# Moving a weight-splitting subtraction from VectorE to GpSimd in the mixer of a one-core decoder step

## The chip, the core and the metric

The kernel runs on one core of one Trainium2 chip. Its time is the device time of one execution in microseconds (us); runs are told by their median. The engines are named as in the profile: PE (TensorE's matmuls), PEld (its weight loads), DVE (VectorE), ACT (ScalarE), POOL (GpSimd) and SP (the queue that issues all DMAs here). Every engine works through its own instructions strictly in the order of the program, so an instruction that waits holds up all that stand behind it on that engine.

## The reference

One step of a decoder layer for 1024 prompt tokens and 8 sample tokens (D = 1024, feed-forward width 2816). The four parts follow each other, each with a residual and a layer norm:

```python
h = LN(ALPHA * h + 0.5 * swiglu(h, ffn1_wi, ffn1_wo))
proj = h @ w_in                      # 58 column tiles of 128
# RWKV-7 branch: token shift, decay, in-context rates, matrix state per head, read out in chunks of 64
# RG-LRU branch: causal convolution of width 4, gates, linear scan, GeLU gate
merged = gate0 * rwkv_out + gate1 * lru_out
h = LN(ALPHA * h + merged @ w_mix_out)
h = LN(ALPHA * h + cross_attention(h, mem_k, mem_v))
h = LN(ALPHA * h + 0.5 * swiglu(h, ffn2_wi, ffn2_wo))
```

All values are float32, and the results must have close to float32 precision.

## The kernel before

Every large product is made of three matmuls (`mm3`, lines 125 to 127): both operands are split into a rounded high part and the rest, and high x high, high x low and low x high are added up in PSUM. So every weight tile must be split before PE can use it. `split_half` does this for half a tile (128 x 512 values): SP loads it into a tile `raw` (line 94), ACT rounds it to `wh` (line 99), DVE subtracts to get `wl` (line 100), and PE takes `wh` and `wl` as the stationary operand. Nothing else sets the pace of the split: the next load into `raw` waits until `wl` is made.

The mixer is the middle part of the program. It first makes the low-rank inputs of the RWKV branch; then (from line 734 on) it works in 16 units, two for each of 8 pairs of heads. In each unit `rounds` interleaves, step by step and in the order of the code, several streams:

- `gemms`: the products with the remaining 52 tiles of `w_in`, in three column groups of 344 tokens (PSUM tile `g`), whose results go out to DRAM as `ev`; in the last two units `out_proj` with the 8 tiles of `w_mix` takes its place;
- `chain`: the recurrence over chunks of 64 tokens. One chunk is a closed chain of PE and DVE (L1049 PE, L1051 DVE `wsb`, L1055 PE, L1061 DVE and an ACT copy into `QZ`, L1065 and L1067 PE, L549 DVE `QZ<-y`), and the next chunk needs its result;
- `inverse`: 31 rounds of a DVE product (`pr<-tq,iv`) and a DVE reduction (L900) that need no PE at all;
- `stage`, `branch`, `post`, `samples_*`: elementwise work for the next unit and the finished one, with small POOL instructions (a power for each norm, L754 `ivs` and `ivc`, and a copy, L845 `BN`).

In this stretch the weights have one `raw` buffer and three pairs of `wh` and `wl`. After the 16 units the last chain, the second part of the output product (`out_last`), the layer norm, the memory's keys and values (`memory_kv`) and the first queries of the attention are interleaved. The scheduler that builds the program may change the order of neighbouring instructions, by its own estimates of when each is ready.

Of the kernel before, what the change touches and what calls it, by code (L numbers as in the profile page):

```python
# [10 lines left out]
F32 = mybir.dt.float32  # L11
F32R = mybir.dt.float32r
AF = mybir.ActivationFunctionType
ALU = mybir.AluOpType
# [20 lines left out]
def weave(*streams):  # L35

    live = [[0.0, i, g, 1.0 / n] for i, (g, n) in enumerate((s if isinstance(s, tuple) else (s, 1) for s in streams))]
    while live:
        x = min(live, key=lambda v: v[:2])
        try:  # L40
            new = next(x[2])
            x[0] += x[3]
            if new:
                live.append([x[0], len(streams), new[0], (1.0 - min(x[0], 0.9)) / new[1]])
        except StopIteration:
            live.remove(x)


def rounds(n, streams, late, keep):


    done = [0] * len(streams)
    for r in range(1, n + 1):
        for g in late[:]:
            try:
                next(g)
            except StopIteration:
                late.remove(g)
        for i, (g, steps) in enumerate(streams):
            while done[i] < steps and (done[i] < steps * r // n or r == n):  # L60
                done[i] += 1
                try:
                    new = next(g)
                    if new:
                        late.append(new[0])
                except StopIteration:
                    done[i] = steps
    for g, steps in streams:
        for new in g:
            if new:  # L70
                late.append(new[0])
    while late and not keep:
        for g in late[:]:
            if next(g, 0) == 0:
                late.remove(g)
# [10 lines left out]
def raw_tile(S):  # L86
    return next(S.rawseq).tile([128, 2 * HN], F32, tag="raw", name="raw")


def split_half(S, src, nm="w", hp=None, view=lambda t: t, to=None):  # L90

    nc = S.nc
    raw = raw_tile(S)[:, :512]
    S.wdma.dma_start(out=view(raw), in_=src)
    if to is None:
        hp = hp or next(S.hlseq)
        to = [hp.tile([128, 512], F32R, tag=nm + x, name=nm + x) for x in "hl"]
    hi, lo = to
    nc.scalar.activation(out=hi, in_=raw, func=AF.Identity)  # L99
    nc.vector.tensor_tensor(out=lo, in0=raw, in1=hi.bitcast(F32), op=ALU.subtract)  # L100
    return hi, lo


def load_split(S, src, nm="w", hp=None):

    return [split_half(S, src[:, 512 * i:512 * i + 512], nm, hp) for i in range(2)]
# [368 lines left out]
def setup(ctx, tc, I):  # L475
    nc = tc.nc
    S = SimpleNamespace(tc=tc, nc=nc, pend=[])
    S.const = ctx.enter_context(tc.tile_pool(name="const", bufs=1))
    S.hp = ctx.enter_context(tc.tile_pool(name="hp", bufs=1))
    S.wraw = ctx.enter_context(tc.tile_pool(name="wraw", bufs=1))  # L480
    S.whl = ctx.enter_context(tc.tile_pool(name="whl", bufs=3))
    S.wdma = nc.sync
    S.dram = ctx.enter_context(tc.tile_pool(name="dram", bufs=1, space=bass.MemoryType.DRAM))
    S.ones_d = S.const.tile([128, 128], F32, name="ones_d")
    nc.vector.memset(S.ones_d, 1.0 / D)
    S.lng = S.const.tile([128, 4, KT], F32, name="lng")
    S.lnb = S.const.tile([128, 4, KT], F32, name="lnb")
    nc.sync.dma_start(out=S.lng, in_=I["ln_g"])
    nc.sync.dma_start(out=S.lnb, in_=I["ln_b"])
    S.mhalf = S.const.tile([128, 8], F32, name="mhalf")  # L490
    nc.vector.memset(S.mhalf, -0.5)
    S.ident = S.const.tile([128, 128], F32, name="ident")
    nc.sync.dma_start(out=S.ident, in_=I["cst"][:, 0:128])
    S.HH = S.hp.tile([128, KT, NT], F32R, name="HH")
    S.HL = S.hp.tile([128, KT, NT], F32R, name="HL")
    return S
# [42 lines left out]
def mixer(octx, S, I, O, MG, HD, pre):  # L539
# [5 lines left out]
    nc, tc = S.nc, S.tc  # L545
# [7 lines left out]
    with ExitStack() as ctx:  # L553
# [107 lines left out]
        with ExitStack() as c2:  # L661
# [64 lines left out]
            def rest():  # L726
                for x in tiles(0)[2:4]:
                    yield from project(0, *x, load_split(S, I["w_in"][x[0]]), CH3, psl, lp)
                ends(0, True)

            weave((first(), 31), *pre)
            weave((low_out(), 29), (rest(), 17))
        S.norms.close()
        S.rawseq, S.hlseq = itertools.cycle([S.wraw]), itertools.cycle([S.whl])

        pools.update(dict.fromkeys(("g", "ch", "y"), ctx.enter_context(tc.tile_pool(name="mps", bufs=1, space=PSUM))))
# [7 lines left out]
        def tmp(tag, n=264, bufs=1, pool=None):  # L744
            return (pool or (t1 if tag in LATE else ta)).tile([128, n], F32, tag=tag, name=tag, bufs=bufs)
# [252 lines left out]
        def direct(k, c0, n, e):  # L998

            ACT(S.HH[:, k, c0:c0 + n], e)  # L1000
            TTo(S.HL[:, k, c0:c0 + n], e, S.HH[:, k, c0:c0 + n].bitcast(F32), ALU.subtract)
# [132 lines left out]
        def samples_c(p, P):  # L1134

            col = lambda t: t[:, p:p + 1]
            y, sg = P.y8, P.sg
            e0 = tmp("e0", 8, 2, t1)
            nc.sync.dma_start(out=e0, in_=GD[p][:, G0, NP:NT])
            while len(P.lm) < 4:  # L1140
                yield
            v = tmp("w8", 8, 2, t1)
            q = psm(8)
            nc.tensor.matmul(q, ones64, y, start=True, stop=True)
            TTo(y, y, q, ALU.subtract)
            ACT(v, y, AF.Square)
            yield
            q = psm(8)
            nc.tensor.matmul(q, ones64, v, start=True, stop=True)
            TSC(v, q, GN_EPS, None, ALU.add, None)  # L1150
            nc.gpsimd.tensor_tensor(out=v, in0=v, in1=mhalf, op=ALU.pow)
            STT(sg[:, 1, :], e0, 1.0, sg[:, 1, :], ALU.add, ALU.mult)
            yield
            yield
            STT(y, y, col(V["gng"]), v, ALU.mult, ALU.mult)
            STT(y, y, col(V["gnb"]), sg[:, 0, :], ALU.add, ALU.add)
            STT(y, y, 0.5, sg[:, 1, :], ALU.mult, ALU.mult)
            STT(y, sg[:, 2, :], 0.5, y, ALU.mult, ALU.add)
            if p < S.npairs - 1:
                nc.sync.dma_start(out=MG[p, :, NP:NT], in_=y)  # L1160
            else:
                direct(p, NP, NS, y)
# [75 lines left out]
        for t in range(nu):  # L1238
# [21 lines left out]
            if t == nu - 1:  # L1260
                s.append((out_proj(range(4, 8), KT - 1, (KT - 2,)), 37))
            rounds(26, s, late_steps, t < nu - 2)
        weave(samples_c(S.npairs - 1, Ps[-1]))
        actx.close()
        S.norms = Norms(S, octx)
        more_weights(S, ctx, 2, 1)
        wp = ctx.enter_context(tc.tile_pool(name="wmix", bufs=3))
        fp = ctx.enter_context(tc.tile_pool(name="fmix", bufs=2))
        w = [[split_half(S, I["w_mix"][4 * i:4 * i + 4, :, 128 * k:128 * k + 128].rearrange("m p c -> p m c"), hp=wp,
                         view=lambda t: t.rearrange("p (m c) -> p m c", c=128)) for i in range(2 if k == KT - 1 else 1)]  # L1270
             for k in (KT - 2, KT - 1)]
# [21 lines left out]
def memory_kv(S, ctx, I, O, psg):  # L1293
# [26 lines left out]
    for c in range(4):  # L1320
        q = psg(512).rearrange("p (t c) -> p t c", c=256)
        for kp in range(4):
            wh, wl = split_half(S, I["wv"][4 * c + kp])
            for k, t in itertools.product(range(2), range(2)):
                T, C = slice(128 * t, 128 * t + 128), slice(256 * k, 256 * k + 256)
                k = 2 * kp + k
                mm3(nc, q[:, t], (mh[:, k, T], ml[:, k, T]), wh[:, C], wl[:, C], k == 0 and t == 0, k == KT - 1 and t == 1)
            yield
        for i in range(2):
            t = pool.tile([128, 256], F32, tag="mi", name="vo")  # L1330
            nc.scalar.activation(out=t, in_=q[:, i], func=AF.Identity)
            for to in (S.VD, O["mv"]):
                nc.sync.dma_start(out=to[i, :, 256 * c:256 * c + 256], in_=t)
        yield
# [318 lines left out]
```

## Time and profile before

| | us |
|---|---|
| median of 3 runs | 3232.01 |
| lowest and highest run | 3231.0 and 3237.26 |
| profiled execution | 3221.89 |
| its span, first to last instruction | 3220.1 |
| PE busy in the span | 3089.7 |
| DVE busy | 2242.6 |
| ACT busy | 1448.6 |
| POOL busy | 556.5 |

Busy time is the union of an engine's instructions. Matmuls overlap in the record, so a busy PE is not a PE at its peak; the idle time of its weight loads (PEld) tells more of where it waits.

### The profile page before, as it was taken

The numbers are of one execution on the slowest core, as the hardware profiler recorded it, in microseconds if no ns is written. First come the engines' busy times: TensorE is split into PE (matmuls) and PEld (weight loads), VectorE is DVE, ScalarE is ACT, GpSimd is POOL, SyncE is SP. The second block draws the span as 40 slices with busy tenths as digits, with TensorE's granted clock in tenths as the row PEclk, the third lists the DMA queues.
The fourth block names the chain that finished last, engine by engine and source line by source line (L and its number), as shares of the span: only waits on it lengthen the run. The fifth ranks groups of instructions, "written<-read, shape, count | busy, mean of one in ns | idle before, by whom it ended". The sixth has DMA issues, their size and how long they took to land. (4 is left out here: it accounts for less than half of the span.)

```text
span 3220.1 us, 63093 instructions
## 1 busy us (share of the span) xinstructions
PE 3089.7 (96%) x23312; PEld 2881.4 (89%) x23312; DVE 2242.6 (70%) x6072; ACT 1448.6 (45%) x3252; POOL 556.5 (17%) x526
## 2 busy tenths in 40 slices
PE   8999999999999999999999999989888999999997
PEld 8999999998798888888888878778887999999997
DVE  7666665574568888777788877676768666666556
ACT  5333352125546565656566565354235433334112
POOL 2222200132000101001010110251005322220111
PEclk9999999999999999999999989889999999999998
DMA  4222253313644444443444444553433222224321
GB/s 137 77 83 76 80 161 107 111 46 138 203 122 126 118 120 120 121 128 108 133 120 120 127 129 130 171 176 123 157 118 116 79 80 80 80 80 157 107 86 53
DMA packets 361078, 370.73 MB, mean 115 GB/s; under 512 B 141728, under 2 KB 259904, under 8 KB 360768
## 3 DMA queue, kind: packets, MB, share of 16 engines
q1 hardware_dynamic: 360768, 366.69, 37.9%
q8 instruction: 183, 3.00, 0.4%
q14 instruction: 127, 1.04, 0.1%
HBM read 269.42 MB, written 97.37 MB: 114 GB/s over the span
## 5 line engine op out<-in xcount | busy, mean ns | idle before, releaser
L125 PE MATMUL ps<-HH,wh 128*128 128x258 f32 (+1 forms) x2384 | 718.6, 302 | 16.8 <-ACT HH L508 7.3
L126 PE MATMUL ps<-HL,wh 128*128 128x258 f32 (+1 forms) x2384 | 717.0, 301 | 0.5 <-POOL HL L215 0.4
L127 PE MATMUL ps<-HH,wl 128*128 128x258 f32 (+1 forms) x2384 | 716.0, 300 | 0.0
L125 PE MATMUL g<-HH,wh 128*128 128x344 f32 (+2 forms) x1840 | 632.4, 344 | 20.1 <-ACT wh L99 4.6
L126 PE MATMUL g<-HL,wh 128*128 128x344 f32 (+2 forms) x1840 | 591.6, 322 | 0.5 <-POOL HL L215 0.3
L127 PE MATMUL g<-HH,wl 128*128 128x344 f32 (+2 forms) x1840 | 588.0, 321 | 0.1
L125 PEld LDWEIGHTS ps<-HH,wh 128*128 128x128 f32 x2384 | 451.7, 190 | 18.9 <-ACT HH L508 7.3
L126 PEld LDWEIGHTS ps<-HL,wh 128*128 128x128 f32 x2384 | 451.2, 189 | 1.3 <-POOL HL L215 0.7
L127 PEld LDWEIGHTS ps<-HH,wl 128*128 128x128 f32 x2384 | 450.7, 189 | 0.0
L125 PEld LDWEIGHTS g<-HH,wh 128*128 128x128 f32 x1840 | 352.6, 192 | 49.9 <-ACT wh L99 6.7
L126 PEld LDWEIGHTS g<-HL,wh 128*128 128x128 f32 x1840 | 353.3, 192 | 5.6 <-POOL HL L215 1.4
L127 PEld LDWEIGHTS g<-HH,wl 128*128 128x128 f32 x1840 | 351.8, 191 | 5.5 <-DVE wl L100 2.1
L228 ACT ACTIVATE wh<-raw 128x512 fp32r<-128x512 f32 x280 | 176.5, 631 | 323.5 <-PE ps L126 263.4
L334 POOL TENSOR_TENSOR raw<-raw 128x512 f32<-128x512 f32 x160 | 213.6, 1335 | 567.4 <-DVE wl L229 352.2
L229 DVE TENSOR_TENSOR wl<-raw,wh 128x512 fp32r<-128x512 f32 x280 | 207.9, 743 | 139.0 <-ACT wh L228 132.2
L99 ACT ACTIVATE wh<-raw 128x512 fp32r<-128x512 f32 x301 | 184.8, 626 | 231.6 <-PE ps L126 89.8
L100 DVE TENSOR_TENSOR wl<-raw,wh 128x512 fp32r<-128x512 f32 x301 | 217.2, 729 | 100.4 <-ACT wh L99 98.3
L442 DVE SCALAR_TENSOR_TENSOR acc<-ps,acc 128x344 f32<-128x344 f32 x336 | 167.9, 512 | 140.7 <-PE ps L127 140.2
L546 DVE TENSOR_TENSOR pr<-tq,iv 128x2 f32<-128x2 f32 (+30 forms) x496 | 160.7, 324 | 2.7
L551 ACT ACTIVATE ev<-g 128x344 f32<-128x344 f32 x192 | 87.2, 455 | 105.5 <-PE g L127 96.9
L900 DVE TENSOR_REDUCE tq<-pr 128x1 f32<-128x2 f32 (+30 forms) x496 | 121.1, 244 | 2.6
L754 POOL TENSOR_TENSOR ivc<-ivc,mhalf 128x4 f32<-128x4 f32 x32 | 33.7, 1054 | 515.1 <-DVE ivc L549 395.1
(417 smaller groups left out, 6623.6 us busy)
## 6 DMA issues: line engine op xcount, KB each, us to landing
raw<-in_wi_dram SPq DMA_DIRECT2D x176, 256.0 KB
raw<-in_w_in_dram SPq DMA_DIRECT2D x116, 256.0 KB
GD<-ev SPq DMA_DIRECT2D x168, 172.0 KB
raw<-in_wo_dram SPq DMA_DIRECT2D x104, 256.0 KB
raw<-HID SPq DMA_DIRECT2D x88, 258.0 KB
HID<-g SPq DMA_DIRECT2D x80, 258.0 KB
row<-T SPq DMA_DIRECT2D x80, 128.0 KB
GD<-t SPq DMA_DIRECT2D x24, 344.0 KB
```

The costliest lines, as they stand in the source:

```text
L99: nc.scalar.activation(out=hi, in_=raw, func=AF.Identity)
L100: nc.vector.tensor_tensor(out=lo, in0=raw, in1=hi.bitcast(F32), op=ALU.subtract)
L125: nc.tensor.matmul(ps, wh, xh, start=first, stop=False)
L126: nc.tensor.matmul(ps, wh, xl, start=False, stop=False)
L127: nc.tensor.matmul(ps, wl, xh, start=False, stop=last)
L228: nc.scalar.activation(out=hi, in_=x, func=AF.Identity)
L229: nc.vector.tensor_tensor(out=lo, in0=x, in1=hi.bitcast(F32), op=ALU.subtract)
L334: pool_tt = lambda o, a, b, op: nc.gpsimd.tensor_tensor(out=o, in0=a, in1=b, op=op)
L442: nc.vector.scalar_tensor_tensor(out=a, in0=q, scalar=0.5 / ALPHA, in1=a, op0=ALU.mult, op1=ALU.add)
L546: TTo = lambda o, a, b, op: nc.vector.tensor_tensor(out=o, in0=a, in1=b, op=op)
L551: ACT = lambda o, a, f=AF.Identity, **kw: nc.scalar.activation(out=o, in_=a, func=f, **kw)
L900: nc.vector.tensor_reduce(out=tq[:, 0:m, i], in_=pv, axis=mybir.AxisListType.X, op=ALU.add)
```

## The change

`split_half` no longer names VectorE for the subtraction but an engine held in `S.low`. It is VectorE at the start, GpSimd from the beginning of the mixer's 16 units to the end of the last one, and VectorE again after that. The layer norm's and the attention's splits and the feed-forward parts are not touched.

```diff
     hi, lo = to
     nc.scalar.activation(out=hi, in_=raw, func=AF.Identity)
-    nc.vector.tensor_tensor(out=lo, in0=raw, in1=hi.bitcast(F32), op=ALU.subtract)
+    S.low.tensor_tensor(out=lo, in0=raw, in1=hi.bitcast(F32), op=ALU.subtract)
     return hi, lo
...
     S.wdma = nc.sync
+
+    S.low = nc.vector
...
         S.norms.close()
+        S.low = nc.gpsimd
         S.rawseq, S.hlseq = itertools.cycle([S.wraw]), itertools.cycle([S.whl])
...
         weave(samples_c(S.npairs - 1, Ps[-1]))
+        S.low = nc.vector
         actx.close()
```

120 subtractions change their engine (52 tiles of `w_in` and 8 of `w_mix`, two halves each). The line numbers of what follows in the file rise by 2 to 4.

On POOL, in the middle of the mixer, the rows before are only the small powers and copies of the streams (the numbers name buffers):

```order
L754 TENSOR_TENSOR ivs_16068<-ivs_16068,mhalf_75 128x4
L845 COPY BN_16243<-BN_16243 64x4x64
L754 TENSOR_TENSOR ivc_16493<-ivc_16493,mhalf_75 128x4
L754 TENSOR_TENSOR ivs_16513<-ivs_16513,mhalf_75 128x4
L845 COPY BN_16685<-BN_16685 64x4x64
```

In the changed program the same stretch of POOL's queue reads:

```order
L757 TENSOR_TENSOR ivs_16068<-ivs_16068,mhalf_75 128x4
L100 TENSOR_TENSOR wl_16112<-raw_16109,wh_16111 128x512
L848 COPY BN_16243<-BN_16243 64x4x64
L100 TENSOR_TENSOR wl_16118<-raw_16115,wh_16117 128x512
L100 TENSOR_TENSOR wl_16363<-raw_16360,wh_16362 128x512
L100 TENSOR_TENSOR wl_16369<-raw_16366,wh_16368 128x512
L100 TENSOR_TENSOR wl_16623<-raw_16620,wh_16622 128x512
L757 TENSOR_TENSOR ivc_16493<-ivc_16493,mhalf_75 128x4
L757 TENSOR_TENSOR ivs_16513<-ivs_16513,mhalf_75 128x4
L100 TENSOR_TENSOR wl_16629<-raw_16626,wh_16628 128x512
L848 COPY BN_16685<-BN_16685 64x4x64
```

Six subtractions now stand between the powers and copies, and the power `ivc_16493` stands behind four of them.

On DVE, at the place where the subtraction for `wl_16363` stood between two rounds of the inverse, the rows before are:

```order
L546 TENSOR_TENSOR pr_15960<-tq_15959,iv_15953 128x105
L547 SCALAR_TENSOR_TENSOR lm_16355<-ge_16002,lm_16355 128x256
L900 TENSOR_REDUCE tq_15959<-pr_15960 128x5
L100 TENSOR_TENSOR wl_16363<-raw_16360,wh_16362 128x512
L546 TENSOR_TENSOR pr_15960<-tq_15959,iv_15953 128x132
L549 TENSOR_SCALAR QZ_14777<-y_15947,scl_15944 64x64
```

and in the changed program, between the same two rounds:

```order
L548 TENSOR_TENSOR pr_15960<-tq_15959,iv_15953 128x105
L548 TENSOR_TENSOR cs_16647<-cs_16647,ref_15004 128x256
L903 TENSOR_REDUCE tq_15959<-pr_15960 128x5
L828 COPY dend_15005<-cs_16647 128x4
L548 TENSOR_TENSOR za_16392<-cs_16647,za_16392 128x256
L548 TENSOR_TENSOR pr_15960<-tq_15959,iv_15953 128x132
L551 TENSOR_SCALAR QZ_14777<-y_15947,scl_15944 64x64
```

The subtraction is gone, elementwise work of the next unit has moved up into its place, and the chain's step `QZ_14777` stands behind the same round as before.

On PE the order changes little in the 16 units (no matmul moves by more than a few dozen places), but more behind them. There the last column group of the output product (`g_26958`, `g_26982`) is interleaved with the memory's keys and values (`kv`). Before, `g_26982` stands behind the products for `kv_26629`:

```order
L126 MATMUL kv_26629<-wl_26687,memh_25666 128x256
L127 MATMUL g_26958<-HH_79,wl_25625 128x264
L169 MATMUL ln_26969<-lns_26833,ones_d_69 128x256
L125 MATMUL g_26982<-HH_79,wh_25618 128x264
L126 MATMUL g_26982<-HL_80,wh_25618 128x264
L125 MATMUL kv_26710<-wh_26713,memh_25666 128x256
```

and in the changed program between products for `kv_26548`, which come earlier:

```order
L125 MATMUL kv_26548<-wh_26551,memh_25666 128x256
L127 MATMUL g_26958<-HH_79,wl_25625 128x264
L125 MATMUL g_26982<-HH_79,wh_25618 128x264
L126 MATMUL g_26982<-HL_80,wh_25618 128x264
L127 MATMUL g_26982<-HH_79,wl_25619 128x264
L125 MATMUL g_26982<-HH_79,wh_25624 128x264
L126 MATMUL kv_26548<-wl_26552,memh_25666 128x256
```

So the end of the output product is issued more than a hundred matmuls earlier than before.

## Rows read from the trace of the kernel before

**Rows 1.** The page, busy time of each engine (us, share, instructions).

```profile
PE 3089.7 (96%) x23312; PEld 2881.4 (89%) x23312; DVE 2242.6 (70%) x6072; ACT 1448.6 (45%) x3252; POOL 556.5 (17%) x526
```

**Rows 2.** Busy time in two windows: the moved subtractions' stretch, and behind it.

```profile
core 0: us, PE busy (x) PEld busy (x) DVE busy (x) ACT busy (x) POOL busy (x), PEclk, DMA share, GB/s
811.00:2033.00 1222.00, 1193.75 (x9271) 1028.64 (x9269) 936.65 (x3196) 705.39 (x1621) 109.10 (x108) 0.98 0.45 126
2033.00:2430.00 397.00, 351.40 (x2691) 327.27 (x2691) 272.81 (x865) 157.16 (x408) 81.22 (x98) 0.95 0.49 152
```

**Rows 3.** Waits of PEld, 811 to 2033 us: total us, times, longest.

```profile
PEld g L125 <- ACT wh L99: 6.7, 12, 1.6
PEld ch L1049 <- DVE QZ L549: 5.1, 18, 0.6
...
PEld y L751 <- ACT gsq L551: 2.0, 6, 0.5
PEld g L127 <- DVE wl L100: 1.9, 7, 0.3
...
PEld ch L1049 <- DVE AR L546: 0.2, 1, 0.2
```

**Rows 4.** Groups by line, 811 to 2033 us: busy us, mean ns | idle before, releasers.

```profile
L546 DVE TENSOR_TENSOR pr<-tq,iv 128x2 f32<-128x2 f32 (+30 forms) x496 | 160.7, 324 | 2.7
...
L100 DVE TENSOR_TENSOR wl<-raw,wh 128x512 fp32r<-128x512 f32 x120 | 83.2, 693 | 16.5 <-ACT wh L99 15.9 <-issue 0.3
...
L754 POOL TENSOR_TENSOR ivs<-ivs,mhalf 128x4 f32<-128x4 f32 x32 | 34.7, 1084 | 212.7 <-DVE ivs L549 110.8 <-DMA ws<-in_srwkv_dram 83.9 <-DVE tq L900 10.4
...
L754 POOL TENSOR_TENSOR ivc<-ivc,mhalf 128x4 f32<-128x4 f32 x29 | 30.5, 1052 | 479.0 <-DVE ivc L549 359.1 <-ACT ev L551 50.1 <-ACT gr L551 26.5
...
L1051 DVE COPY wsb<-ch 128x64 f32<-128x64 f32 x121 | 26.9, 222 | 36.5 <-PE ch L1049 34.8
...
L845 POOL COPY BN<-BN 64x256 f32<-64x256 f32 x32 | 18.8, 587 | 293.4 <-DVE BN L547 149.6 <-DVE tq L900 82.4 <-DVE pr L546 40.9
```

**Rows 5.** Line 334, whole span: ns min/median/max, first and last start.

```profile
L334 POOL TENSOR_TENSOR raw<-raw x160: 1272/1295/2442, 36.8 to 2900.3; 128x512 f32<-128x512 f32 x160
```

**Rows 6.** Line 333 on DVE, whole span, in the same columns.

```profile
L333 DVE TENSOR_TENSOR g<-g,c x160: 410/428/1537, 84.7 to 2935.3; 128x258 f32<-128x258 f32 x160
...
L333 DVE TENSOR_TENSOR g<-p,ps x40: 410/424/427, 65.0 to 2898.9; 128x258 f32<-128x258 f32 x40
```

**Rows 7.** Timeline of the first feed-forward part: start, length, instruction.

```profile
176.53 2.79 POOL L334 TENSOR_TENSOR raw<-raw 128x512 f32<-128x512 f32 x2 [7.28 <-DVE wl L229]
...
178.21 1.40 DVE L333 TENSOR_TENSOR g<-g,c 128x258 f32<-128x258 f32 x1
...
179.53 0.41 DVE L333 TENSOR_TENSOR u<-u,ps 128x258 f32<-128x258 f32 x1
```

**Rows 8.** Timeline in the mixer.

```profile
954.60 1.35 POOL L845 COPY BN<-BN 64x256 f32<-64x256 f32 x1 [7.71 <-DVE tq L900]
954.81 0.28 DVE L546 TENSOR_TENSOR pr<-tq,iv 128x64 f32<-128x64 f32 x1
...
954.99 0.70 DVE L100 TENSOR_TENSOR wl<-raw,wh 128x512 fp32r<-128x512 f32 x1
```

**Rows 9.** Timeline in the mixer, one half tile of weights.

```profile
1306.20 0.62 ACT L99 ACTIVATE wh<-raw 128x512 fp32r<-128x512 f32 x1
...
1307.27 0.69 DVE L100 TENSOR_TENSOR wl<-raw,wh 128x512 fp32r<-128x512 f32 x1
```

**Rows 10.** Timeline in the mixer, another half tile.

```profile
1332.43 0.63 ACT L99 ACTIVATE wh<-raw 128x512 fp32r<-128x512 f32 x1
...
1339.36 0.68 DVE L100 TENSOR_TENSOR wl<-raw,wh 128x512 fp32r<-128x512 f32 x1
```

**Rows 11.** Waits of PEld, 2033 to 2430 us.

```profile
PEld g L125 <- DVE acc L1488: 8.3, 9, 1.8
```

## Prediction

> **What bounds the kernel now.** I read the page first: PE is busy 3089.7 of 3220.1 us, PEld 2881.4, DVE 2242.6, POOL 556.5 [rows 1]. So PE sets the time, and VectorE's work counts only where PE waits for it. Then I cut the span into windows. The 120 subtractions that move start between 811.0 and 2032.5 us, so the window of 811 to 2033 us (1222 us) is the stretch that matters [rows 2]. In it PE's record is nearly full (1193.75), but the weight loads are busy only 1028.64 us: some 193 us in which PE loads no weights. DVE is busy 936.65 us with 3196 instructions, 77% of the stretch and the highest share after PE; POOL is busy 109.10 us, 9%. This is what makes the move look cheap.
>
> Then I asked what ends PE's waits there, in the view of waits for the weight loads. The rows with DVE as releaser run from 5.1 us for the chain's `QZ` down to 0.2 us; there are 65, and they sum to 52.6 us [rows 3]. That is all that a faster DVE could give back directly. The moved subtraction itself is hardly among them: PE waits for `wl` 1.9 us in 7 waits, and for `wh`, the step before it, 6.7 us in 12 [rows 3]. So the subtraction matters for what stands behind it in DVE's queue, not for its result. The rest of PE's idle time in the stretch (ACT's late results, short gaps between small matmuls) is not the change's to move.
>
> **The change, part by part.** Each term is a change of PE's waiting, in the profiled execution of 3221.89 us; the median of the runs, 3232.01, lies 10.1 us above that, and I add the sum to the median.
>
> *DVE is freed.* 120 subtractions of 693 ns are 83.2 us, and before them DVE stood idle 15.9 us until ACT had made `wh` [rows 4]. Together 99 us. On average PE waits 52.6 us for 936.65 us of DVE work, 0.056 us for each, so this is worth 99 x 0.056 = 5.6 us. That is the even price. If DVE's backlog behaves as a queue, waits go as b/(1-b) with b the busy share: 936.65/1222 = 0.766 gives 3.28, (936.65 - 83.2)/1222 = 0.698 gives 2.31, 30% less, or 15 us. I take 5.6 and keep 15 as the far end.
>
> *DVE is held.* The trace of before has no subtraction of this kind on POOL in the mixer, but it has one of the same shape in the feed-forward part: 1.295 us as median, and up to 2.442 [rows 5]. While it runs, DVE instructions with both inputs in SBUF stretch: `g<-g,c` has a median of 428 ns but a maximum of 1537, while `g<-p,ps`, which takes one input from PSUM, never exceeds 427 [rows 6]. One case in time: two POOL instructions of the line run from 176.53 for 2.79 us, to 179.32; `g<-g,c` starts at 178.21, lasts 1.40, and so ends 0.29 us after them; the next one with a PSUM input takes its usual 0.41 [rows 7]. So a GpSimd subtraction can hold DVE for anything from nothing to 1.295 us. For the middle: DVE starts an instruction each 1222/3196 = 0.38 us, and by the kernel's text about half of them have both inputs in SBUF (the `pr` products alone are 496 of the 3196 [rows 2, 4]), so the first that is held comes after some 0.5 us and loses the other 0.8. That is 120 x 0.8 = 96 us, at the even price +5.4 us. Ends: nothing, and 120 x 1.295 = 155 us; the queue's price for that is (853.5 + 155)/1222 = 0.825, b/(1-b) 4.72 against 3.28, or +23 us. I take 0.8 because rows 7 show that the hold lasts to the end of the POOL instruction.
>
> The Trainium skill (SBUF — State Buffer, "Who interferes with whom") speaks against this change: a VectorE instruction with two SBUF inputs contends with a GpSimd instruction that reads SBUF, and whichever is issued first has the shared port for its whole instruction. Rows 6 and 7 agree, with 1537 against 428 ns. By the rule the sum would be the held end above, and not an offload for nothing.
>
> Freed and held come to -0.2 us: the offload is eaten by the port.
>
> *The weights.* Today `wl` is late because DVE's queue is: in one case `wh` ends at 1306.82 and `wl` at 1307.96, 1.14 us later [rows 9]; in another 1333.06 and 1340.04, 7 us later [rows 10]. GpSimd has little in its queue and needs 1.295 us, so it is 0.16 us later in the first case, far earlier in the second; the next load into `raw` then starts as much earlier. PE waits for `wl` come in cases like the first: 7 x 0.16 = +1 us. Ends: both waits gone, -8.6; or each of the 19 waits longer by 1.295 - 0.693 = 0.60, +11.4. What hides the rest is that three pairs of buffers let the splits run ahead of the products.
>
> *GpSimd's queue.* 155 us of subtractions in 1222 are a chance of 0.127 that a power finds one running, with half of 1.295 left: 0.08 us for each of the 61 powers `ivs` and `ivc` [rows 4], 5 us in all. ACT waits behind them; PE waited for `gsq` in 6 of 29 cases [rows 3, 4], one in five, so +1 us; ends 0 and +5. Where several subtractions stand ahead of a power, as ahead of `ivc_16493`, it can be more; that is a rival below.
>
> *The order behind the mixer.* Nothing is added there, but the end of the output product is issued over a hundred matmuls earlier, and the memory's products later. In 2033 to 2430 us PE's largest wait of this kind is 8.3 us, for `acc` of L1488 [rows 11]. A shift of up to that either way is possible, and I see no sign for it: 0, ends -8.3 and +8.3.
>
> The sum is -0.2 + 1 + 1 + 0 = +1.8 us: 3223.7 for a profiled execution like this one, and 3232.0 + 1.8, about **3234 us**, as a median. This is no change that can be told: a measurement of this kernel tells 0.2%, 6.5 us.
>
> **The rivals.** *Slower: the hold lands in front of the chain.* Each chunk has four DVE instructions (one `wsb`, one `QZ` copy, two halves of `QZ<-y`); 121 chunks [rows 4] make 484, one each 2.5 us. They read PSUM and are not held themselves, but they queue behind one that is. 0.8/2.5 = 32% of 120 holds are 38 chain steps, each late by up to 0.8 us, +30; against this the old 0.69 us stood in front of 33 steps, late by half of it, 11.5 us. So it decides when more than (6.5 + 11.5)/38 = 0.47 us of a hold passes to PE. For it: the chain is where PE's DVE waits are. Against: the longest of them now is 0.6 us [rows 3], so other matmuls cover most. At +14 it gives 3246; chance 0.21.
>
> *Slower: powers queue behind several subtractions* that wait for `wh`. If 8 of the 61 stand behind four (5.2 us), that is 42 us of ACT time, a fifth of it for PE: +8, 3240; chance 0.08.
>
> *Faster: GpSimd is the one that waits.* At 954.60 us the copy `BN` takes 1.35 us (mean 0.587), while DVE runs `pr` in 0.28 and the subtraction in 0.70, undisturbed [rows 4, 8]. If DVE's two-input work, which follows back to back in the mixer, mostly keeps GpSimd out, the held term goes to nothing and the freed one stays, between -5.6 and -15; with the weights no later, -10: 3222. Against it: rows 7. Chance 0.26.
>
> **How the numbers follow.** No change that can be told has 0.45, the slower rivals 0.21 + 0.08 = 0.29, the faster one 0.26. The range must reach into both rivals: 3216 (the freed end of 15 us) to 3254 (the held end of 23 us, eased by 1); within 0.2% of 3232 alone would be 3226 to 3238.
>
> **What would show it.** Right: POOL shows line 100 x120 at 1.3 us or a little above; POOL is busy some 265 us in the stretch; DVE's busy time there stays near 936 because `pr` and the other two-input products grow (`pr` from a mean of 324 ns to some 360), while `wsb` stays at 222 [rows 4]; DVE's part of PEld's waits stays near 52 us. If DVE's busy time falls to 855 and `pr` stays at 324, the faster rival holds, and line 100 on POOL will be well over 1.3 us. If the chain's waits (L1049, L1055, L1065) grow by 10 us or more, the first slower one does; if PE's waits for `gsq` and `s` do, the second. A difference that lies behind 2033 us is the order's, and would make the sum right only by chance.

## The result, and the profile after

| | before | after |
|---|---|---|
| median of 6 runs each, side by side, us | 3231.51 | 3255.93 |
| lowest and highest run | 3223.89 and 3237.26 | 3244.65 and 3262.72 |
| span of the profiled execution | 3220.1 | 3242.9 |

The ratio is 1.009, with a 95% interval of 1.0065 to 1.0116: the change makes the kernel slower by 24 to 29 us (the difference of the medians, and the ratio). The prediction had 3234 and a range up to 3254.

The page of the kernel after, busy time of each engine:

```profile
PE 3082.9 (95%) x23312; PEld 2878.1 (89%) x23312; DVE 2261.0 (70%) x5952; ACT 1450.3 (45%) x3254; POOL 723.5 (22%) x646
```

DVE has 120 instructions fewer than in [rows 1] and is busy 18.4 us longer. The windows show where; the first one holds the moved subtractions, the second what follows (columns as in [rows 2]):

```profile
811.00:2053.00 1242.00, 1184.30 (x9229) 1024.28 (x9227) 950.28 (x3070) 705.30 (x1615) 271.29 (x227) 0.98 0.44 125
2053.00:2452.00 399.00, 351.78 (x2722) 326.55 (x2720) 277.44 (x870) 156.48 (x412) 84.23 (x99) 0.95 0.49 149
```

The first window has 20 us more than in [rows 2] for nearly the same work less the subtractions (PE has 42 matmuls fewer in it); the second is the stretch behind it, as long as before but for 2 us. So the loss lies inside the 16 units. The groups by line in the first window, which answer to [rows 4]:

```profile
L548 DVE TENSOR_TENSOR pr<-tq,iv 128x2 f32<-128x2 f32 (+30 forms) x496 | 199.2, 402 | 4.1
...
L100 POOL TENSOR_TENSOR wl<-raw,wh 128x512 fp32r<-128x512 f32 x119 | 163.5, 1374 | 562.9 <-ACT wh L99 486.8 <-PE y L1063 29.0 <-DMA sg<-GD 14.5
...
L1054 DVE COPY wsb<-ch 128x64 f32<-128x64 f32 x120 | 26.7, 222 | 46.5 <-PE ch L1052 44.2
```

The products `pr`, with both inputs in SBUF, go from a mean of 324 to 402 ns; `wsb`, which reads PSUM, stays at 222. That is the hold on VectorE. DVE's busy time is a union, and its instructions overlap in the record (before, count times mean over all lines of this window sums to 1117.7 us, the union is 936.65), so the size of the hold is read from the sums: without the 120 subtractions 1034.5 us before and 1118.6 after. VectorE's other instructions were lengthened by some 84 us.

PE's waits grow; of the view of waits of the weight loads in the first window, which answers to [rows 3]:

```profile
PEld y L754 <- ACT gsq L553: 16.3, 15, 2.6
PEld ch L1052 <- DVE QZ L551: 9.8, 17, 3.3
PEld m L969 <- DVE ku L548: 8.8, 14, 1.1
PEld g L127 <- POOL wl L100: 8.2, 12, 0.9
PEld y L1068 <- DVE QZ L1064: 5.1, 8, 1.6
```

Two kinds of wait have grown. The chain's `QZ` and `ku` are DVE's. The largest, `gsq`, was 2.0 us and is 16.3: that is a norm's square, made by ACT behind a DVE subtraction.

To compare kernels I use one stretch with the same work in each, from the start of the first `wsb` to the start of the last (128 chunks). Before, after, and the last `wsb` against the span: 3220.1 - 2092.3 = 1127.8 us follow it before, 3242.9 - 2114.7 = 1128.2 after. The tile's rows of the two:

```profile
L1051 DVE COPY wsb<-ch x128: 211/224/226, 939.5 to 2092.3; 128x64 f32<-128x64 f32 x128
```

```profile
L1054 DVE COPY wsb<-ch x128: 210/224/229, 943.9 to 2114.7; 128x64 f32<-128x64 f32 x128
```

So nothing is lost behind the mixer, and 18 of the profile's 22.8 us are in this stretch (4.4 more in the lead up to it).

### The profile page after: what moved, and what is told of

The parts are those of the page before. It is cut to its first block, busy times and chain, and to the rows that moved or that the text cites. A ratio compares the mean times of both kernels' runs of the same rounds, so it can differ in the third digit from the quotient of the medians.

```text
span 3242.9 us, 63160 instructions
## 1 busy us (share of the span) xinstructions
PE 3082.9 (95%) x23312; PEld 2878.1 (89%) x23312; DVE 2261.0 (70%) x5952; ACT 1450.3 (45%) x3254; POOL 723.5 (22%) x646
## 5 line engine op out<-in xcount | busy, mean ns | idle before, releaser
L334 POOL TENSOR_TENSOR raw<-raw 128x512 f32<-128x512 f32 x160 | 214.2, 1339 | 566.5 <-DVE wl L229 363.5
L229 DVE TENSOR_TENSOR wl<-raw,wh 128x512 fp32r<-128x512 f32 x280 | 204.0, 729 | 140.3 <-ACT wh L228 133.4
L100 POOL TENSOR_TENSOR wl<-raw,wh 128x512 fp32r<-128x512 f32 x120 | 164.8, 1373 | 608.5 <-ACT wh L99 532.3
L548 DVE TENSOR_TENSOR pr<-tq,iv 128x2 f32<-128x2 f32 (+30 forms) x496 | 199.2, 402 | 4.1
L100 DVE TENSOR_TENSOR wl<-raw,wh 128x512 fp32r<-128x512 f32 x181 | 135.0, 756 | 69.7 <-ACT wh L99 67.7
L464 POOL TENSOR_TENSOR acc<-acc,raw 128x516 f32<-128x516 f32 x32 | 42.8, 1341 | 420.4 <-DVE acc L442 419.5
```

The lines of the kernel that those rows point to most:

```text
L100: S.low.tensor_tensor(out=lo, in0=raw, in1=hi.bitcast(F32), op=ALU.subtract)
L229: nc.vector.tensor_tensor(out=lo, in0=x, in1=hi.bitcast(F32), op=ALU.subtract)
L334: pool_tt = lambda o, a, b, op: nc.gpsimd.tensor_tensor(out=o, in0=a, in1=b, op=op)
L464: nc.gpsimd.tensor_tensor(out=a, in0=a, in1=x, op=ALU.add)
L548: TTo = lambda o, a, b, op: nc.vector.tensor_tensor(out=o, in0=a, in1=b, op=op)
```

## The experiments

The change does two things: the subtraction runs on another engine, and the scheduler makes another order of everything else. To part them, a kernel is built twice. From the first build the order of every engine is read; in the second each instruction is tied behind the one before it in that list, without a semaphore. A subtraction that isn't on the listed engine goes in where the scheduler puts it. "Old order" is that of before, "new order" that of the changed kernel. Differences below are ratio times 3226 us. The line numbers in these kernels are 30 to 54 higher.

```diff
+            if last is not None and i.engine == last.engine:
+                tc.add_manual_dep(i, last.name, info, reason="order")
...
-        S.low = nc.gpsimd
+        S.low = getattr(nc, CASE["low"])
```

### Engine alone and order alone

e1, old order, subtraction on GpSimd:

```diff
+    nc = program('gpsimd', _order(program('vector', None)))
```

> The 120 subtractions run on GpSimd as in the changed kernel, but every engine keeps the order of its other instructions from the kernel before. If the port (a GpSimd subtraction holding VectorE) or late weights cost the time, this is as slow as the changed kernel: +20 us or more over the kernel before, with `pr` at a mean near 400 ns. If the new order costs it, this is within 6 us of the kernel before.

e2, new order, subtraction on VectorE:

```diff
+    nc = program('vector', _order(program('gpsimd', None)))
```

> The mirror: every engine keeps the order of the changed kernel, but the 120 subtractions run on VectorE again. If the order costs the time, +20 us or so over the kernel before, with PE's waits for `gsq` near 16 us as in the changed kernel. If the port or late weights do, within 6 us of the kernel before, with `pr` back at 324 ns.

Measured: e1 1.0064 (1.0042 to 1.0086), +21 us; e2 1.0084 (1.0063 to 1.0106), +27 us. Each half of the change costs nearly as much as the whole, and together they are not the sum. Neither the engine nor the order is innocent. Taken one behind the other, the engine costs 21 us in the old order (e1), and the new order 8 us on top of that (the changed kernel against e1; the two intervals overlap).

A hold in e1, from the timeline (start, length, instruction):

```profile
882.36 1.29 POOL L130 TENSOR_TENSOR wl<-raw,wh 128x512 fp32r<-128x512 f32 x1 [8.52 <-ACT wh L129]
...
882.51 1.18 DVE L578 TENSOR_TENSOR pr<-tq,iv 128x16 f32<-128x16 f32 x1
```

The round of `pr` over 14 columns just before took 0.18 us; this one, over 16, takes 1.18 and ends at 883.69, 0.04 us after GpSimd at 883.65.

### The hold: freeing VectorE without it, and with it but for nothing

e3, old order, the subtraction in the mixer's 16 units cut to one column on VectorE (the condition keeps the full one elsewhere); the low parts of the weights are left out:

```diff
-    S.low.tensor_tensor(out=lo, in0=raw, in1=hi.bitcast(F32), op=ALU.subtract)
-    return hi, lo
+    if not S.use_high or CASE["plain"]:
...
+    S.low.tensor_tensor(out=lo[:, 0:1], in0=raw[:, 0:1], in1=hi.bitcast(F32)[:, 0:1], op=ALU.subtract)
+    return hi, hi
```

> Order of the kernel before; the subtraction in the mixer's stretch is cut to one column on VectorE, and the products there take the high part a second time in place of the low part, so the result lacks the weights' low parts. It shows what freeing VectorE is worth without any hold. The prediction's even price: 5 us faster than the kernel before; its far end: 15 us faster. If PE hardly waits behind the subtraction, no change.

e4, the same with the full subtraction on GpSimd, whose result nobody reads:

```diff
+    if not S.use_high or CASE["plain"]:
...
     S.low.tensor_tensor(out=lo, in0=raw, in1=hi.bitcast(F32), op=ALU.subtract)
-    return hi, lo
+    return hi, hi
```

> As the run without low parts, but GpSimd makes the whole low part at the old order and no product reads it, so no matmul can wait for it. If the hold of VectorE (and GpSimd's queue) is the cost, this is as slow as the run with the old order and GpSimd, some 20 us over the kernel before. If late weights are the cost, it is no slower than the run without low parts, that is 0 to 15 us faster than the kernel before.

Measured: e3 0.9959 (0.9944 to 0.9975), -13 us; e4 1.0058 (1.0036 to 1.008), +19 us. The difference, 32 us by the ratios and 30.6 by the medians, is the hold, with what GpSimd's longer instruction delays besides it (the next load into `raw`, GpSimd's queue). e4 lies as high as e1, so that late weights cost nothing that can be told apart from the rest. The 128-chunk stretch of e3 and of e4 (the columns of [rows 2]):

```profile
938.20:2081.90 1143.70, 1121.92 (x8856) 965.55 (x8856) 851.31 (x3073) 656.00 (x1504) 119.56 (x123) 0.97 0.46 128
```

```profile
937.70:2119.20 1181.50, 1141.38 (x8856) 976.41 (x8856) 911.92 (x2967) 654.28 (x1503) 262.01 (x229) 0.96 0.44 124
```

and of before:

```profile
939.50:2092.30 1152.80, 1125.23 (x8856) 964.80 (x8857) 897.77 (x3074) 656.20 (x1504) 121.70 (x123) 0.97 0.45 127
```

The length less PEld's busy time is the time in which PE loads no weights, called PE's idle time from here on: 188.0 us before, 178.2 in e3, 205.1 in e4. From before to e3 DVE's busy time falls by 46.5 us and PE's idle time by 9.8, which is 0.21 for each. From e3 to e4 DVE's busy time rises by 60.6 and PE's idle time by 26.9, which is 0.44 for each. e3's one-column instructions (165 ns) blur this. In e6, told below, nothing stands in their place, and GpSimd has none of its 120 instructions in this stretch; e6, and then e1:

```profile
942.70:2085.70 1143.00, 1121.19 (x8856) 966.00 (x8857) 842.84 (x2968) 656.31 (x1504) 120.85 (x123) 0.97 0.46 128
```

```profile
937.90:2106.40 1168.50, 1128.03 (x8856) 962.32 (x8856) 911.89 (x2967) 655.11 (x1504) 263.95 (x229) 0.97 0.45 125
```

PE's idle time is 177.0 us in e6. From before to e6 it falls by 11.0 for 54.9 us less of DVE (0.20 for each); from e6 to e4 it rises by 28.1 for 69.1 us more (0.41 for each). So a held microsecond costs twice what a freed one gives, and some seven times the 0.056 of the prediction. The granted clock, 0.96 against 0.97, adds to e4's time; e1, at 0.97, has much the same idle time, 206.2 us.

The price also has a part that 0.056 left out, since that counted only waits that DVE ended. In this stretch the rows with DVE as releaser sum to 58.8 us before, 53.7 in e6 and 70.1 in e4, those with ACT as releaser to 31.0, 23.3 and 36.0. So 0.24 of the 0.41 are DVE's rows, and most of the rest is ACT's. How much of ACT's part came from held DVE instructions was not followed: `wh` (3.5 us more in e4 than in e6) can also be late because the load into `raw` now waits for GpSimd.

### What on GpSimd holds VectorE

All in the old order, 120 times on GpSimd, unread, as in e4, with the low parts left out. e6 writes zeros, e7 copies one operand, e11 subtracts half the columns:

```diff
+    S.low.memset(lo.bitcast(F32), 0.0)                                      # e6
+    S.low.tensor_copy(out=lo, in_=raw)                                      # e7
+    S.low.tensor_tensor(out=lo[:, 0:256], in0=raw[:, 0:256], in1=hi.bitcast(F32)[:, 0:256], op=ALU.subtract)  # e11
```

> The order of before; GpSimd writes zeros over the low tile (128x512) 120 times in place of the subtraction, reads nothing, and nobody reads the result; the third products take the high part, so the low parts are left out. Theory (VectorE is held while GpSimd reads SBUF): no hold, as the old order with the one-column subtraction, -18 to -8 us, mean of pr 320 to 335 ns. Rival (the cost is GpSimd's writing or its place in GpSimd's queue): +8 us or more, pr over 360 ns.

> The order of before; GpSimd copies the raw weight into the low tile (one SBUF operand read in place of two), 120 times, and nobody reads the result; the third products take the high part, so the low parts are left out. Theory (the hold comes with any reading by GpSimd, and its price follows the time that the 120 instructions take): if a copy takes 0.6 us or more, at least a third of the 30.6 us between the unread subtraction and none, so -3 to +12 us against before, pr 345 to 400 ns. Rival (only two operands hold): -18 to -8 us, pr under 335 ns.

> The order of before; 120 times GpSimd subtracts the first 256 of the 512 columns, which nobody reads, and the third products take the high part, so the low parts are left out. Theory (two SBUF operands on GpSimd hold VectorE for as long as the instruction runs): about half of the 30.6 us between the unread full subtraction and the one-column one, so some +3 us against before, -4 to +9, mean of pr 350 to 385 ns. Rival (it was the length of the instruction and not its two operands: the copy of 0.71 us held nothing, so this one of about the same length doesn't either): -18 to -8 us, pr under 342 ns.

| | mean on GpSimd, ns | mean of `pr`, ns | ratio to before | us |
|---|---|---|---|---|
| e3, none | | 327 | 0.9959 (0.9944 to 0.9975) | -13 |
| e6, zeros, all ahead of the first `pr` | 541 | 325 | 0.9957 (0.9936 to 0.9979) | -14 |
| e7, copy | 714 | 340 | 0.9963 (0.9947 to 0.9979) | -12 |
| e11, 256 columns subtracted | 791 | 351 | 0.9987 (0.9967 to 1.0007) | -4 |
| e4, 512 columns subtracted | 1339 | 413 | 1.0058 (1.0036 to 1.008) | +19 |

Of the table, from the groups by line of e6 and e11:

```profile
L582 DVE TENSOR_TENSOR pr<-tq,iv 128x2 f32<-128x2 f32 (+30 forms) x496 | 161.3, 325 | 4.1
...
L133 POOL MEMSET wl<- 128x512 f32 x119 | 58.7, 541 | 0.7
```

```profile
L582 DVE TENSOR_TENSOR pr<-tq,iv 128x2 f32<-128x2 f32 (+30 forms) x496 | 174.0, 351 | 4.1
...
L133 POOL TENSOR_TENSOR wl<-raw,wh 128x256 fp32r<-128x256 f32 x120 | 95.0, 791 | 660.2 <-ACT wh L129 600.2 <-DMA GD<-t 45.1 <-issue 14.9
```

e6 does not test what it was made for. The zeros read nothing, so they did not wait for a weight: all 120 ran between 810.3 and 876.6 us, and the first `pr` starts at 883.3 (views by tile):

```profile
L133 POOL MEMSET wl<- x120: 517/522/716, 810.3 to 876.6; 128x512 f32 x120
```

So its time and its `pr` are those of a VectorE that is freed and not held. They meet the theory's numbers, but show nothing of a write beside the chain; that rival stays untested there. What e6 does show lies in the window of 810 to 877 us, in which GpSimd was busy for 63.01 of 67 us. Two-input instructions of VectorE took as long as in e3, but one with a single input was lengthened. e6, and then e3:

```profile
L585 DVE TENSOR_SCALAR t<-t 128x344 f32<-128x344 f32 x13 | 6.4, 496 | 1.0 <-ACT t L587 0.6
...
L582 DVE TENSOR_TENSOR cs<-cs,ref 128x256 f32<-128x256 f32 x3 | 1.3, 418 | 0.0
```

```profile
L585 DVE TENSOR_SCALAR t<-t 128x344 f32<-128x344 f32 x12 | 4.1, 338 | 0.6 <-ACT t L587 0.2
...
L582 DVE TENSOR_TENSOR cs<-cs,ref 128x256 f32<-128x256 f32 x3 | 1.3, 419 | 0.0
```

The copies of e7 do stand all through the stretch, so 120 more places in GpSimd's queue and as many writes of 714 ns cost 1 us against e3, which is within the intervals. For the copy the rival was right in the time, and `pr` at 340 lies between the two. In e11 `pr` is at the theory's lower end and the time at its lower end too; the interval alone (-11 to +2 us) would not exclude the rival, and by the medians e11 is 7 us faster than before. What the table shows is that the loss rises with the lengthening of `pr` (in time only e4 is clear of the other rows), and that this grows faster than the instruction's length: half the columns give 24 of the 86 ns. Between 714 and 791 ns one operand more and 11% more time cannot be told apart as causes.

### Dose, and which subtractions

e8 puts every second subtraction on GpSimd. e9 and e10 put 48 there: those during which VectorE's instructions were lengthened least, and most, in e1 and e4. All are in the old order and leave nothing out.

```diff
+    next(S.lows).tensor_tensor(out=lo, in0=raw, in1=hi.bitcast(F32), op=ALU.subtract)    # e8
...
+    low = S.low if S.nlow in TAKEN else nc.vector                                         # e9, e10
+    low.tensor_tensor(out=lo, in0=raw, in1=hi.bitcast(F32), op=ALU.subtract)
```

> The order of before; every second subtraction is made by GpSimd, the other half by VectorE; nothing is left out. Theory (each hold has a price of its own, so the loss goes with their number): half of +19.6 us, 6 to 14 us. Rival (a few late results are hidden, and the loss begins only when many holds follow one another): 4 us or less, or a gain.

> The order of before; 48 of the 120 subtractions are GpSimd's, those during which VectorE's instructions were lengthened least in the two old-order runs with all 120 on GpSimd (14.9 us in their sum of 82.5); the other 72 stay on VectorE. Nothing is left out. Theory (the price is that of the held time: the 12.5 us that VectorE gave when all 120 were gone, so 5.0 us for 48, against 30.6 us for 82 us held, so 5.5 us for 14.9): about 0 us, -6 to +5. Rival (the number of GpSimd subtractions or their late weights decides, whichever they are): two fifths of +19.6 us, about +8, and the same as the run with the 48 most held.

> As the run before, with the 48 subtractions during which VectorE was held most (48.0 us in their sum). Nothing is left out. Theory: -5.0 + 17.9 = about +13 us, 7 to 19, and 8 us or more above the run with the 48 least held. Rival (the number decides): about +8 us, the same as that run.

Measured: e8 1.0017 (1.0 to 1.0035), +5 us, which doesn't tell its two theories apart; e9 1.0002 (0.9985 to 1.002), +1 us; e10 1.0046 (1.0026 to 1.0066), +15 us. The same number of subtractions costs 14 us more where VectorE is held. `pr` and the subtractions in e9, and then in e10:

```profile
L586 DVE TENSOR_TENSOR pr<-tq,iv 128x2 f32<-128x2 f32 (+30 forms) x496 | 172.3, 347 | 3.0
...
L137 POOL TENSOR_TENSOR wl<-raw,wh 128x512 fp32r<-128x512 f32 x48 | 62.3, 1299 | 418.8 <-ACT wh L134 399.4 <-PE y L1109 10.4 <-PE g L164 7.6
```

```profile
L586 DVE TENSOR_TENSOR pr<-tq,iv 128x2 f32<-128x2 f32 (+30 forms) x496 | 185.3, 374 | 3.4
...
L137 POOL TENSOR_TENSOR wl<-raw,wh 128x512 fp32r<-128x512 f32 x48 | 65.7, 1368 | 265.3 <-ACT wh L134 250.6 <-PE g L164 9.7 <-PE y L1102 5.0
```

This is the clearest of the runs: the number of subtractions on GpSimd does not set the price, and the held time goes with it. Late weights can be some 4 of the 14 us: over the 128 chunks PE waits for `wl` from GpSimd 0.9 us in e9 and 4.6 in e10, while its idle time is 187.3 and 201.2. Even the best chosen 48 only break even.

### The order

e5 is e3 in the new order:

```diff
+    nc = program('vector', _order(program('gpsimd', None)))
```

> The order of the changed kernel on every engine; the 120 subtractions are cut to one column on VectorE and the third products take the high part in place of the low one, so the low parts are left out. Theory (the order carries a loss of its own, whatever VectorE does): the +26 us of the new order with VectorE's subtraction and the -12.5 us of the old order without it add, some +13 us against before, 8 to 20. Rival (the order is right for a VectorE that is free, and costs only where VectorE is late): as the old order without the low parts, -18 to -8 us, and the PE weight loads that wait for ACT's gsq fall back from 26 us to under 8.

Measured: 0.9991 (0.9975 to 1.0008), -3 us, between the two theories. So the new order loses 10 us against e3 even when VectorE is free, and 27 when it has the subtractions; with the hold it is 8 (after against e1, with intervals that overlap). The waits for `gsq`, the most conspicuous ones, stay. In e5 and then in e2:

```profile
PEld y L789 <- ACT gsq L587: 14.0, 13, 3.1
```

```profile
PEld y L784 <- ACT gsq L583: 22.1, 14, 4.1
...
PEld ch L1082 <- DVE QZ L581: 12.6, 18, 2.7
PEld y L1098 <- DVE QZ L1094: 7.5, 14, 1.8
```

In e2's timeline `gsq` is late where the subtraction that centres `ysb` stands in DVE's queue behind rows that began after its product had ended, up to 9 of them, among them state updates of 0.69 us (`wt`, `ws`). So e12 and e14 take e2, and e13 the changed kernel, and move only that row ahead (e12 one row too far at seven places, which e14 mends). By their edits e12 and e14 move it at 14 places, and e13 at 15, past 49 rows; the expectations of e12 and e13 name 15, and 16 with 64 rows.

```diff
+        if dve[k][1] == "ysb<-ysb,y":
+            ...
+            dve.insert(to, dve.pop(k))
```

> The order of the changed kernel with the subtraction on VectorE (+26 us when nothing else was touched), and on VectorE alone 15 rows are moved: the subtraction that centres ysb goes ahead of the 2 to 10 rows that stood between it and the end of its product in that run's trace. Nothing is left out. Theory (the loss of the order lies there: rows such as wt and ws of 0.69 us ahead of ysb, then gsq and the products that wait 25.8 us for it): gsq's waits fall under 8 us, and 12 to 22 us of the 26 go, so +4 to +14 us against before. Rival (another row of the chain is late by the same time, since those 15 rows only move the wait, or the order's loss lies elsewhere): +18 us or more.

> The changed kernel (+29 us) with the same subtraction of ysb moved ahead of the rows that stood between in its own trace (16 places, 64 rows passed). Nothing is left out. Theory (hold and order each have a price): gsq's waits of 20 us fall under 8, 8 to 16 us go, and what remains is the hold's: +13 to +22 us against before. Rival (the hold alone sets the loss whatever the order): +24 us or more.

> The run e12 again, mended: there the subtraction of ysb stood one row too far ahead at seven places, so that VectorE waited for its product (15.2 us of idle time before that row in all, 8.7 before the move). Here it passes only the rows that began after its product had ended (14 places, 2 to 9 rows). Nothing is left out. Theory, already weakened by e13 (the order's loss lies at that row): +4 to +14 us against before, PE's idle time in the stretch of 128 chunks under 200 us. Rival (the wait moves on to the chain's QZ, and the loss lies elsewhere): +18 us or more, PE's idle time 205 us or more.

Measured: e12 1.0106 (1.008 to 1.0133), +34 us; e14 1.0093 (1.0072 to 1.0114), +30 us, no faster than e2; e13 1.0075 (1.005 to 1.01), +24 us, its interval overlapping that of the changed kernel. The same waits of e14:

```profile
PEld ch L1103 <- DVE QZ L602: 12.8, 19, 2.6
PEld y L1119 <- DVE QZ L1115: 12.3, 19, 1.7
PEld y L805 <- ACT gsq L604: 11.3, 12, 2.7
```

`gsq` gave back 10.8 of its 22.1 us, but the chain's `QZ` (L1098 in e2, L1119 here) took 4.8 of them. The 128-chunk stretch of e2 and of e14:

```profile
939.30:2120.80 1181.50, 1126.05 (x8874) 967.33 (x8875) 901.13 (x3077) 658.68 (x1507) 121.44 (x124) 0.96 0.45 125
```

```profile
941.00:2118.60 1177.60, 1128.25 (x8874) 969.83 (x8875) 903.61 (x3077) 659.06 (x1507) 121.62 (x124) 0.96 0.45 125
```

PE's idle time is 214.2 us in e2 and 207.8 in e14, against 188.0 before. My theory fell: the row in front of `gsq` was where a large wait showed, and a few us come back with it, but not the 27 us of the order. Which rows of the new order cost them stays open. A mixture of one engine's new order with the others' old order was not run.

## Why the prediction was wrong

*What it had right.* PE sets the time, the mixer is the place, and the hold is real and near the predicted size: some 84 us where the sum had 96. POOL's row stands at a median of 1.29 us, as foretold, and POOL's busy time at 271 us (265). The Trainium skill (SBUF — State Buffer, "Who interferes with whom") says that a VectorE instruction with two SBUF inputs contends with a GpSimd instruction that reads SBUF, and not with one that only writes. Both halves agree with the traces: a subtraction there takes `pr` from 327 to 413 ns (e3, e4), and beside e6's zeros `cs<-cs,ref` took 418 ns against 419. The end of the program is unchanged (1127.8 and 1128.2 us), as the term for the order behind the mixer had it. One of its signs of being right failed: DVE's part of PEld's waits, foretold to stay near 52 us, is 67.8 us in the window of the changed kernel (sum of its rows).

*The step that failed: the even price.* "0.056 us for each" is an average over all of DVE's work, and it counts only the waits that DVE ended; ACT's late results were said to be "not the change's to move". *DVE is freed* was put at -5.6 and measured -13 (e3, with one-column subtractions left) and -14 (e6, with none), near the queue's far end of -15; from before to e6 the waits that ACT ended fell by 7.7 us, more than the 5.1 of those that DVE ended. What was freed was also less than the sum's 0.693 us for each subtraction: in e6 DVE's busy time falls by 54.9 us for 106 of them, 0.52 each, since its instructions overlap in the record. *DVE is held* was put at +5.4 and measured +31 (e4 against e3), beyond the queue's far end of +23. Both terms were too small, the held one far more, so that the "-0.2" of freed and held together became +19. A held microsecond cost 0.41 us of PE's idle time, a freed one gave 0.20. One reason for the difference, argued from the rows and not shown by itself: the scheduler gave the subtractions on VectorE a place where it saw room, while a hold strikes whatever VectorE has just begun.

*The rival that came nearest.* The first slower one has a hold land in front of the chain. Its price, +14, has the right sign but is short of the +21 of e1. The longest wait of `ch` for `QZ` was 0.6 us before and is 1.2 in e1, and these waits come to 10.3 us instead of 5.1; here are the rows of e1:

```profile
PEld ch L1082 <- DVE QZ L581: 10.3, 27, 1.2
PEld g L157 <- POOL wl L130: 8.3, 15, 1.0
PEld y L1098 <- DVE QZ L1094: 5.7, 18, 0.7
PEld y L784 <- ACT gsq L583: 3.9, 6, 0.9
```

By the sign that the prediction set for it (the chain's waits grow by 10 us or more) it falls short: over the 128 chunks all waits of the chain's three lines sum to 92.7 us before, 98.1 in e1 and 97.0 in the changed kernel. Those of them that DVE ended grow by 7.5 us in e1, where PE's idle time grows by 18.2. So the chain is a part of the price, not all of it.

*The weights.* `wl` on GpSimd now ends waits of 8.3 us (1.9 before), inside the term's far end. Yet e4, where no product waits for them, is no faster than e1: there the products wait for `wh` 7.3 us over the 128 chunks (3.8 in e1), so these waits stand in place of others.

*GpSimd's queue.* `gsq` waits 3.9 us in e1 (2.0 before): +2 where the term had +1. The second slower rival is not it; the 16.3 us in the changed kernel are the order's.

*The order inside the 16 units* had no term at all: "no matmul moves by more than a few dozen places" was taken for harmless. It costs 27 us with the subtractions on VectorE (e2), 10 with none (e5 against e3), and in the changed kernel some 8 on top of e1. In e2 the waits that grew most are for `gsq` and `QZ`, which stand behind VectorE; that VectorE's moved rows and not PE's cost the time is argued from this, and not shown.

*The faster rival* (GpSimd is the one that waits) fell: `pr` grew, and e3 and e6 show that 13 to 14 us were all that an offload of this work could give in the old order.

## What to carry to other kernels

A microsecond of an engine beside the bound has no one price: here one taken off VectorE was worth 0.20 us of PE's idle time, one added by a hold cost 0.41, and the average over its work said 0.056. Before moving two-operand elementwise work to GpSimd, look at what VectorE does in the same stretch; if that is two-operand work with PE's recurrence behind it in the queue, the hold can cost more than the offload frees, as it did here. Look in the trace, too, at when the instructions of an experiment ran: e6's zeros had all ended before the work that they were to disturb began. And when an edit also reorders the program, run it once with the old order and once with the new order alone: both halves may cost.

## What the runs showed of the hardware

GpSimd's instruction of 128x512 took a mean of 541 ns for zeros, 714 for a copy and 1339 for a subtraction, where VectorE subtracts in 693. Zeros written by GpSimd did not lengthen VectorE's two-input instructions (418 ns against 419), but took the one-input `t<-t` from 338 to 496 ns (e6 against e3, 810 to 877 us). The copy, which does read SBUF, lengthened `pr` by only 13 ns on average and cost 1 us against e3 within the intervals, against 86 ns and 32 us for the subtraction: I had expected the loss to go with the length of the instruction.
